# Closing products and norms by token, and a 31-tap convolution as dense products

## The chip, the cores and the metric

One NeuronCore of one Trainium2 chip. The metric is the device time of one execution in microseconds, median of three runs.

## The reference

512 tokens of 1024 channels, float32. Four blocks follow one another on one residual stream `x`; each adds two branches, `x = x + rms_norm(branch(rms_norm(x)))`. Blocks 1 and 2 have a mixer of three gated branches and a gated FFN with a 3-tap convolution (2 x 2816 hidden channels). Block 3 is a Conformer convolution module and an FFN, block 4 attention over dilated keys and an FFN. The parts that the change touches:

```python
def rms_norm(x, g):
    y = x * lax.rsqrt(jnp.mean(x * x, axis=-1, keepdims=True) + EPS)
    return y * g

def conformer_conv_module(h, w_in, b_in, dw, dw_b, ln_g, ln_b, w_out, b_out):
    u = h @ w_in + b_in
    u = u[..., :D_MODEL] * jax.nn.sigmoid(u[..., D_MODEL:])
    u = causal_dwconv(u, dw, dw_b)          # 31 taps, each channel by itself
    u = layer_norm(u, ln_g, ln_b)
    u = jax.nn.silu(u)
    return u @ w_out + b_out

x = x + rms_norm(y, post_gain)              # y: the closing product of a branch
h = rms_norm(x, pre_gain)                   # the next branch reads h
```

## The kernel before

**Layout.** Everything is held by feature: `x`, `y` and `h` are tiles of 128 features (partitions) x 8 feature tiles x 512 tokens. A product takes a 128 x 128 weight tile as stationary operand and streams the tokens. For accuracy weights and activations are split into a high and a low fp32r part, and `mm3` (line 318) makes each product of three matmuls: high x high, high x low, low x high. Attention, the convolution's taps, sums and transposes are plain fp32 matmuls.

**Weights** come in units of 8 tiles (128 x 1024, 512 KB) from one array in the order of a plan. `dma_to` (270) loads a unit on SP into one of three raw buffers, `split_to` (274) splits it, high on ACT (295) and low on DVE (296), into four rotating buffers or, where the plan says keep, into a second set of four. Units of two stages get the norm's gain multiplied in on GpSimd first (292).

**Order.** `spend` and `tick` keep a modelled clock: generators (lanes) for norms, softmaxes and taps are resumed when that clock passes the time that they asked for, so their instructions fall between the products. The framework below then orders each engine's instructions with the program's order as priority.

**Closing** (`closing`, 557). The last product of a branch (8 tiles of k, 8 tiles of output features) is done for tokens 0 to 255 and then for 256 to 511, 256 columns a matmul. Tiles 4 to 7 are kept for the second half, tiles 0 to 3 are loaded again. `close_tile` (519) evacuates each tile, ACT squares it, and GpSimd adds the squares up (381). In an FFN 14 of 22 k tiles were summed into `y` before, by `close_group` (497), 512 columns a matmul.

**Norms** (`norms`, 446). For each half: `rstd` (386) sums over features with 1-column matmuls (367), takes the reciprocal root in eleven small DVE instructions (`inv_sqrt`, 342, with the scaling at 393), and spreads it over the partitions with two PE transposes (358); `post_norm` (422) scales `y`, adds it to `x`, squares; a second `rstd`; `pre_norm` (403) scales `x` (413), ACT makes the high part (416), DVE and GpSimd the low part (418).

**Head** (`head`, 462). The first six output tiles of the next stage are done in halves too, so that half 0 can run while half 1 is normed: 288 matmuls of 256 columns.

**Convolution** (`conv_inputs`, 1156). For each of 16 half tiles the 31 taps are shared out by hand: ACT scales and GpSimd adds some (1201, 1202), PE does some as products with a diagonal matrix that ACT builds (1215, 1226), DVE does the rest (1245). `layer_norm` (1121) follows by half, with the same token sums.

## Time and profile before

| | us |
|---|---|
| median of 3 runs (3381.99 to 3386.56) | 3386.5 |
| the profiled execution's own time | 3382.53 |
| its span, first to last instruction | 3380.8 |
| PE busy (its matmuls) | 3249.0 |
| DVE, ACT, GpSimd busy | 1970.3, 1391.9, 725.0 |

The page gives one profiled execution. PE is TensorE's matmuls, PEld its weight loads, DVE VectorE, ACT ScalarE, POOL GpSimd, SP SyncE, which issues the loads. Matmuls overlap one another in the records, so a rate is read from a stretch and the number of matmuls in it, not from the duration of one; an fp32 matmul has two records, an fp32r matmul and a transpose one.

### The profile page before, as it was taken

Reading aid. Unit: us, or ns where it says so; the run is one execution under the profiler, and the core shown is the slowest. Engines: PE = TensorE matmul, PEld = TensorE weight load, DVE = VectorE, ACT = ScalarE, POOL = GpSimd, SP = SyncE. Lnnn points to the kernel's source line nnn. Section 1 sums busy time; section 2 is a strip of 40 time slices with the busy share of each in tenths; the row PEclk is TensorE's granted clock in tenths of the full one; section 3 lists DMA queues with packets and bytes.
Section 4 is the critical chain, followed back from the end, with each engine's and each line's share of the span. In section 5 each row is a group of like instructions: output and inputs, shape, how many; then the busy total and the mean of one; then the engine's idle time right before and its main releaser. Section 6 shows DMA issues by size and latency. Waiting matters only on the chain.

```text
span 3380.8 us, 45518 instructions
## 1 busy us (share of the span) xinstructions
PE 3249.0 (96%) x17626; PEld 2786.9 (82%) x17626; DVE 1970.3 (58%) x3697; ACT 1391.9 (41%) x2394; POOL 725.0 (21%) x753
## 2 busy tenths in 40 slices
PE   7999999999999999999998869999999999999998
PEld 7887888888988778988897668888888888898888
DVE  6655347455775443655567988455754454474555
ACT  4443244334454333444345655333433333353333
POOL 1122122000311212300024553000433333230001
PEclk9999999999999999999998979999999999999999
DMA  3111232222321223322231112232312222133222
GB/s 131 63 64 59 87 113 82 100 97 97 113 66 57 67 68 101 105 89 99 94 126 59 35 44 83 99 100 94 125 60 79 82 75 81 63 102 105 100 94 94
DMA packets 85848, 291.56 MB, mean 86 GB/s; under 512 B 9728, under 2 KB 16128, under 8 KB 85632
## 3 DMA queue, kind: packets, MB, share of 16 engines
q1 hardware_dynamic: 84480, 287.60, 25.6%
q8 instruction: 139, 2.28, 0.3%
q10 hardware_dynamic: 1152, 1.05, 0.1%
q14 instruction: 77, 0.63, 0.1%
HBM read 286.52 MB, written 2.10 MB: 85 GB/s over the span
## 4 chain that ended last, share of the span: by engine, by line
PE 81%; DVE 12%; POOL 2%; issue 2%; ACT 2%; DMA 1%; SPq 0%; POOLq 0%; DVEq 0%; ACTq 0%
PE mm L325 23%; PE mm L326 22%; PE mm L327 22%; DVE v L1245 4%; DVE w L296 2%; POOL acc L381 2%; PE z L326 1%; PE z L327 1%; PE z L325 1%; PE wpo L985 1%; PE ss L367 1%; DMA raw<-in_wall 1%; PE pt L862 1%; PE wsc L955 1%; PE dpo L1349 1%
## 5 line engine op out<-in xcount | busy, mean ns | idle before, releaser
L325 PE MATMUL mm<-hh,w 128*128 128x512 f32 (+1 forms) x2720 | 1058.5, 390 | 1.6 <-DVE cv L612 1.6
L326 PE MATMUL mm<-hl,w 128*128 128x512 f32 (+1 forms) x2720 | 1037.7, 382 | 0.0
L327 PE MATMUL mm<-hh,w 128*128 128x512 f32 (+1 forms) x2720 | 1037.4, 382 | 0.0
L296 DVE TENSOR_TENSOR w<-raw,w 128x1024 fp32r<-128x1024 f32 x468 | 605.1, 1293 | 439.7 <-ACT w L295 439.3
L295 ACT ACTIVATE w<-raw 128x1024 fp32r<-128x1024 f32 x468 | 492.5, 1053 | 274.1 <-PE mm L327 203.6
L325 PEld LDWEIGHTS mm<-hh,w 128*128 128x128 f32 x2720 | 513.1, 189 | 101.4 <-issue 12.9
L327 PEld LDWEIGHTS mm<-hh,w 128*128 128x128 f32 x2720 | 513.5, 189 | 98.7 <-issue 1.4
L326 PEld LDWEIGHTS mm<-hl,w 128*128 128x128 f32 x2720 | 514.5, 189 | 89.5 <-issue 2.4
L381 POOL TENSOR_TENSOR acc<-acc,sq 128x256 f32<-128x256 f32 x180 | 174.2, 974 | 1437.5 <-ACT sq L384 1412.2
L612 DVE SCALAR_TENSOR_TENSOR cg<-mm,vecs,cg 128x511 f32<-128x511 f32 (+1 forms) x176 | 131.9, 749 | 205.1 <-ACT cg L605 202.4
L325 PE MATMUL mm<-ah,w 128*128 128x512 f32 (+1 forms) x704 | 249.1, 357 | 1.1 <-ACT ah L632 0.9
L326 PE MATMUL mm<-al,w 128*128 128x512 f32 (+1 forms) x704 | 249.2, 354 | 0.0
L327 PE MATMUL mm<-ah,w 128*128 128x512 f32 (+1 forms) x704 | 248.7, 354 | 0.0
L612 DVE SCALAR_TENSOR_TENSOR cv<-mm,vecs,cv 128x511 f32<-128x511 f32 (+1 forms) x176 | 131.8, 749 | 100.3 <-ACT cv L605 97.8
L292 POOL TENSOR_TENSOR raw<-raw,vecs 128x1024 f32<-128x1024 f32 x72 | 146.1, 2030 | 199.5 <-DMA raw<-in_wall 193.9
L605 ACT ACTIVATE cg<-mm,vecs 128x512 f32<-128x512 f32 x88 | 68.4, 777 | 275.9 <-PE mm L327 275.9
L325 PEld LDWEIGHTS mm<-ah,w 128*128 128x128 f32 x704 | 135.0, 192 | 21.4 <-ACT ah L632 4.1
L326 PEld LDWEIGHTS mm<-al,w 128*128 128x128 f32 x704 | 135.4, 192 | 18.5 <-DVE al L633 1.6
L326 PE MATMUL mm<-hl,keep 128*128 128x256 f32 x512 | 146.9, 290 | 3.7 <-POOL hl L418 3.7
L327 PEld LDWEIGHTS mm<-ah,w 128*128 128x128 f32 x704 | 135.4, 192 | 17.2
L327 PE MATMUL mm<-hh,keep 128*128 128x256 f32 x512 | 146.6, 290 | 0.0
L325 PE MATMUL mm<-hh,keep 128*128 128x256 f32 x512 | 145.1, 294 | 1.5 <-ACT hh L416 1.5
(292 smaller groups left out, 5364.5 us busy)
## 6 DMA issues: line engine op xcount, KB each, us to landing
raw<-in_wall SPq DMA_DIRECT2D x532, 512.0 KB, 3.3
x<-in_x SPq DMA_DIRECT2D x4, 512.0 KB, 6.8
bt<-in_rpb SPq DMA_DIRECT2D x16, 128.0 KB, 2.0
out<-x SPq DMA_DIRECT2D x8, 128.0 KB, 1.8
out<-x ACTq DMA_DIRECT2D x8, 128.0 KB, 1.8
vecs<-in_vecs SPq DMA_DIRECT2D x1, 598.0 KB, 6.0
wpool<-in_w_pool SPq DMA_DIRECT2D x2, 256.0 KB, 2.7
cos<-in_cos SPq DMA_DIRECT2D x2, 256.0 KB, 2.9
```

The source lines that it names most:

```text
L292: nc.gpsimd.tensor_tensor(rows, rows, g[:, k0 : k0 + n, None].to_broadcast(list(rows.shape)), op=OP.mult)
L295: nc.scalar.activation(hi, raw, AF.Copy)
L296: nc.vector.tensor_tensor(lo, raw, hi.bitcast(F32), op=OP.subtract)
L325: nc.tensor.matmul(ps, wh, xh, start=first and i == 0, stop=False, **check)
L326: nc.tensor.matmul(ps, wh, xl, start=False, stop=False, **check)
L327: nc.tensor.matmul(ps, wl, xh, start=False, stop=stop, **check)
L367: self.nc.tensor.matmul(ps[:, i : i + 1], x[:, i * P : (i + 1) * P], self.ones, start=n == 0, stop=n == len(parts) - 1, skip_group_check=True,
L381: self.nc.gpsimd.tensor_tensor(parts[0], parts[0], sq, op=OP.add)
L605: nc.scalar.activation(o, ps, AF.Identity, scale=self.vec(taps + str(k0), f), bias=self.vec(cb, f))
L612: nc.vector.scalar_tensor_tensor(o[:, to], ps[:, of], self.vec(taps + str(k), f), o[:, to], op0=OP.mult, op1=OP.add,)
L862: nc.tensor.transpose(pt[:, k * P : (k + 1) * P], pm[:, k * P : (k + 1) * P], self.ident)
L1245: nc.vector.scalar_tensor_tensor(to, u, w, pss[n] if k == n_pool else to, op0=OP.mult, op1=OP.add)
```

## The change

Closing products have the token tile as stationary operand and stream 512 output columns, so `y` and `x` lie by token (128 tokens x 4 x 1024 features). All eight weight units of a closing stay for both halves. `x` is loaded and stored by token; the gains and one bias that act behind a closing product come as rows spread over the partitions by one load each (`row`). Norm sums are `accum_out` of ACT's squares, `x` gets its update in one DVE instruction a token tile, and the normed stream is transposed on PE into the layout of `h`. `head` takes its weight units one at a time and works tile by tile. The convolution is made of dense products: tokens are split in four residues by 4, a partition is a residue and one of 32 channels, and a 128 x 128 matrix that GpSimd builds from the taps and a 32 x 32 identity does four residues of one step; nine steps make the 31 taps. The input gets into that layout by 16 small copies a tile on SP's queue. Layer-norm sums come from `bn_stats` by token. `inv_sqrt`, `mm3`, `gemm`, `dma_to`, `split_to` and the FFN's own work are as before; SiLU and its split now follow a transpose back.

The diff, cut:

```diff
-BEGIN = 3
+CONV_M, CONV_PAD = 9, 8
+BEGIN = 4
+NORM_SUM, NORM_NEXT, NORM_TILE = (2.2, 3.6), 7.0, 1.1
...
     def closing(w, l, kt):
         _, last = out_groups(kt)
-        add(gemm_tiles(w, l, range(4), last))
-        add(gemm_tiles(w, l, range(4, 8), last), keep=True)
-        add(gemm_tiles(w, l, range(4), last))
+        for n, k in enumerate(last):
+            add(gemm_tiles(w, l, range(8), [k]), keep=n >= 4)
...
+    def rms(self, sums):
+        v = self.sm.tile([P, 2], F32, tag="var", name="var", bufs=2)
+        y = self.sm.tile([P, 2], F32, tag="rst", name="rst", bufs=4)
+        nc.vector.tensor_tensor(v, sums[:, :, 0], sums[:, :, 1], op=OP.add)
+        nc.vector.tensor_scalar(v, v, 1.0 / D, EPS, op0=OP.mult, op1=OP.add)
+        self.inv_sqrt(y, v)
+        return y
+
+    def square(self, x, total):
+        junk = self.sp.tile([P, S], F32, tag="junk", name="junk")
+        self.nc.scalar.activation(junk, x, AF.Square, accum_out=total)
+
+    def norms(self, h, banks, y, add, gain, bias, pre):
+        sums = self.sm.tile([P, 2, 2], F32, tag="sums", name="sums", bufs=4)
+        for i in range(2):
+            for n in range(2):
+                cols = slice(n * S, (n + 1) * S)
+                ps, to = banks[i][n], y[:, 2 * h + i, cols]
+                if add:
+                    nc.vector.tensor_tensor(to, to, ps, op=OP.add)
+                    self.square(to, sums[:, i, n : n + 1])
+                elif bias is not None:
+                    nc.vector.tensor_tensor(to, ps, bias[:, cols], op=OP.add)
+                    self.square(to, sums[:, i, n : n + 1])
+                else:
+                    self.square(ps, sums[:, i, n : n + 1])
+                    nc.vector.tensor_tensor(to, ps, gain[:, cols], op=OP.mult)
+                if add or bias is not None:
+                    nc.gpsimd.tensor_tensor(to, to, gain[:, cols], op=OP.mult)
+        rs = self.rms(sums)
+        for i in range(2):
+            t = 2 * h + i
+            for n in range(2) if pre is False else range(1):
+                cols = slice(n * S, (n + 1) * S) if pre is False else slice(0, D)
+                nc.vector.scalar_tensor_tensor(
+                    self.x[:, t, cols], y[:, t, cols], rs[:, i : i + 1], self.x[:, t, cols],
+                    op0=OP.mult, op1=OP.add,
+                )
...
+        yield from self.pre_norm(h, pre)
+
+    def pre_norm(self, h, gain, wait=(0.0, 0.0)):
+        sums = self.sm.tile([P, 2, 2], F32, tag="sums", name="sums", bufs=4)
+        for i in range(2):
+            for n in range(2):
+                cols = slice(n * S, (n + 1) * S)
+                self.square(self.x[:, 2 * h + i, cols], sums[:, i, n : n + 1])
+        rs = self.rms(sums)
+        xn = []
+        for i in range(2):
+            xn.append(self.sp.tile([P, D], F32, tag="xn", name="xn", bufs=2))
+            if i:
+                nc.vector.tensor_scalar(
+                    xn[i], self.x[:, 2 * h + i], rs[:, i : i + 1], None, op0=OP.mult
+                )
+            else:
+                nc.scalar.activation(xn[i], self.x[:, 2 * h + i], AF.Copy, scale=rs[:, i : i + 1])
+        yield NORM_SUM[h] + NORM_NEXT
+        for f in range(0, KD, 2):
+            pt = self.psum("b", "htp")
+            for j in range(2):
+                for i in range(2):
+                    nc.tensor.transpose(
+                        pt[:, (2 * j + i) * P : (2 * j + i + 1) * P],
+                        xn[i][:, (f + j) * P : (f + j + 1) * P], self.ident,
+                    )
...
+                for j in range(2):
+                    self.split_out(
+                        self.hh[:, f + j, at], self.hl[:, f + j, at], pt[:, j], self.vec(gain, f + j)
+                    )
+            self.ready[h] = f + 2
+            yield NORM_TILE
...
+    def mm3_rows(self, ps, x, w, first, last):
+        (xh, xl), (wh, wl) = x, w
+        nc.tensor.matmul(ps, xh, wh, start=first, stop=False)
+        nc.tensor.matmul(ps, xh, wl, start=False, stop=False)
+        nc.tensor.matmul(ps, xl, wh, start=False, stop=last)
...
+    def close_some(self, xs, units, banks, h, ks, which, first, last):
+        for k in ks:
+            rows = [half.rearrange("p n m -> p (n m)") for half in units[k]]
+            for i, n in which:
+                cols = slice((2 * h + i) * P, (2 * h + i + 1) * P)
+                self.mm3_rows(
+                    banks[i][n], (xs[k][0][:, cols], xs[k][1][:, cols]),
+                    [r[:, n * S : (n + 1) * S] for r in rows], k == first, k == last,
+                )
...
+            for k in range(done, KD):
+                units += self.take_units(gemm_tiles(w, l, range(8), [last[k]]))
...
+                self.close_some(xs, units, banks, 0, [k], every, 0, KD - 1)
+            self.spawn(self.norms(0, banks, y, add, gain, bias, pre))
+            banks = [[self.psum(tag, "mm") for tag in tags] for tags in (("a", "a"), ("a", "b"))]
+            order = (4, 5, 6, 7, 0, 1, 2, 3)
+            self.close_some(xs, units, banks, 1, order, every, 4, 3)
+            self.spawn(self.norms(1, banks, y, add, gain, bias, pre))
             if pre is not False:
                 self.head()
...
+        def matrices(j):
+            w = self.cf.tile([P, 4, CONV_M, 4, 32], F32, tag="cw", name="cw", bufs=2)
+            for i in range(4):
+                nc.gpsimd.tensor_tensor(
+                    w[:, i],
+                    taps[:, 4 * j + i, :, :, None].to_broadcast([P, CONV_M, 4, 32]),
+                    same[:, None, None, :].to_broadcast([P, CONV_M, 4, 32]),
+                    op=OP.mult,
+                )
...
+            up = cv.tile([P, 4, CONV_PAD + P], F32, tag="cup", name="cup", bufs=3)
+            nc.gpsimd.memset(up[:, :, :CONV_PAD], 0.0)
+            for i in range(4):
+                for q in range(4):
+                    nc.sync.dma_start(
+                        up[32 * q : 32 * q + 32, i, CONV_PAD:], u[32 * i : 32 * i + 32, q]
+                    )
...
+                for i in range(4):
+                    w = mats[j][:, i]
+                    for m in range(CONV_M):
+                        nc.tensor.matmul(
+                            ps[:, i * P : (i + 1) * P], w[:, m].rearrange("p a b -> p (a b)"),
+                            phased[j][:, i, CONV_PAD - m : CONV_PAD - m + P],
+                            start=m == 0, stop=m == CONV_M - 1, skip_group_check=True,
+                        )
...
+                if j + 2 < KD:
+                    matrices(j + 2)
+                vc = cv.tile([P, 4, P], F32, tag="vc", name="vc", bufs=2)
+                nc.vector.tensor_tensor(
+                    vc, ps.rearrange("p (i s) -> p i s", i=4),
+                    bias[:, 4 * j : 4 * j + 4, None].to_broadcast([P, 4, P]), op=OP.add,
+                )
...
+                for i in range(4):
+                    nc.tensor.transpose(pt[:, i * P : (i + 1) * P], vc[:, i], self.ident)
...
+                for q in range(4):
+                    nc.vector.bn_stats(stats[:, q, j], by[:, q])
```

## Rows read from the trace of the kernel before

**Rows 1.** The page's head, its part 1 (busy us, share of the span, instructions of each engine) and one line of its part 2 (the granted TensorE clock in 40 slices).

```profile
span 3380.8 us, 45518 instructions
...
PE 3249.0 (96%) x17626; PEld 2786.9 (82%) x17626; DVE 1970.3 (58%) x3697; ACT 1391.9 (41%) x2394; POOL 725.0 (21%) x753
...
PEclk9999999999999999999998979999999999999999
```

**Rows 2.** PE's waits over the whole execution: who waited for whom, us in total, times, longest.

```profile
PE bc L358 <- DVE rst L353: 29.3, 17, 10.2
PE taps L1226 <- DVE cu L1174: 24.3, 5, 10.4
PE ss L367 <- POOL acc L381: 16.3, 13, 4.1
PE mubc L358 <- DVE mu L1132: 13.8, 1, 13.8
```

**Rows 3.** Nine stretches (of the four plain closings with head the first, the second and the last): us from the span's start, length, then busy time (and instructions) of PE, PE's weight loads, DVE, ACT and GpSimd, granted clock, DMA share, GB/s.

```profile
0.00:61.00 61.00, 43.94 (x308) 43.00 (x309) 36.35 (x94) 24.43 (x46) 12.06 (x21) 0.92 0.46 155
470.00:564.00 94.00, 89.04 (x713) 88.12 (x712) 60.85 (x128) 45.71 (x89) 33.28 (x34) 0.96 0.30 97
848.40:942.10 93.70, 88.60 (x713) 87.55 (x712) 67.56 (x152) 42.49 (x80) 33.07 (x41) 0.96 0.33 108
1729.60:1823.70 94.10, 88.79 (x714) 87.62 (x713) 66.34 (x144) 42.16 (x78) 33.34 (x41) 0.96 0.30 100
1823.70:1998.20 174.50, 124.00 (x533) 102.96 (x531) 169.24 (x287) 114.38 (x280) 108.90 (x117) 0.86 0.10 34
1998.20:2102.10 103.90, 96.88 (x756) 94.41 (x757) 87.65 (x199) 53.41 (x109) 38.22 (x41) 0.95 0.27 87
2385.40:2487.70 102.30, 91.63 (x713) 90.24 (x712) 69.04 (x136) 38.59 (x72) 53.11 (x43) 0.93 0.30 96
2933.40:3036.80 103.40, 96.02 (x788) 94.34 (x787) 74.02 (x178) 51.73 (x110) 36.51 (x41) 0.98 0.26 88
3320.10:3380.80 60.70, 48.92 (x405) 48.14 (x403) 31.89 (x76) 16.22 (x27) 16.03 (x18) 0.92 0.29 92
```

**Rows 4.** PE alone in four stretches that hold one kind of matmul each: products of 512 columns, products of 256 columns, taps of the convolution in a long run, taps behind a wait. Columns as above, PE only.

```profile
2102.20:2145.40 43.20, 43.20 (x192) 1.00 0.31 100
860.70:873.60 12.90, 12.90 (x111) 1.00 0.50 168
1912.00:1956.70 44.70, 44.70 (x195) 0.94 0.06 17
1973.40:1981.60 8.20, 8.20 (x29) 0.68 0.00 1
```

**Rows 5.** Groups of instructions by line and shape, on ACT and then on DVE: count, busy us in all, mean ns of one, idle time before them.

```profile
L416 ACT ACTIVATE hh<-hf 128x256 fp32r<-128x256 f32 x128 | 51.3, 417 | 77.4 <-DVE hf L413 67.3 <-DVE hf L411 9.7
...
L829 ACT ACTIVATION_READ_ACCUMULATOR pm<-sc,smx,rq 128x1 f32 x64 | 12.5, 195 | 0.0
...
L726 ACT ACTIVATE rsq<-mm 128x512 f32<-128x512 f32 x10 | 5.9, 594 | 8.3 <-PE mm L327 8.2
...
L296 DVE TENSOR_TENSOR w<-raw,w 128x1024 fp32r<-128x1024 f32 x468 | 605.1, 1293 | 439.7 <-ACT w L295 439.3
...
L413 DVE SCALAR_TENSOR_TENSOR hf<-x,vecs,bc 128x256 f32<-128x256 f32 x112 | 49.3, 473 | 13.9 <-PE bc L358 13.8
...
L511 DVE TENSOR_TENSOR y<-y,mm 128x512 f32<-128x512 f32 x32 | 22.0, 686 | 38.1 <-PE mm L327 38.1
...
L1342 DVE COPY dps<-dpt 128x128 f32<-128x128 f32 x8 | 2.3, 292 | 15.4 <-PE dpt L1337 15.4
```

**Rows 6.** The same view for PE (taps of the convolution, token sums) and for PE's weight loads (one product of the attention over dilated keys).

```profile
L1226 PE MATMUL taps<-cu,cdiag 128*128 128x256 f32 x246 | 62.0, 415 | 24.3 <-DVE cu L1174 24.3
...
L367 PE MATMUL ss<-ones,acc 128*128 128x1 f32 x240 | 31.5, 250 | 18.6 <-POOL acc L381 16.3 <-ACT acc L384 2.3
...
L1349 PEld LDWEIGHTS dpo<-dps,dv 128*128 128x128 f32 x240 | 35.1, 191 | 3.4
```

**Rows 7.** PE alone in a stretch that holds nothing but fp32 products of 128 columns with weights of their own (two records each).

```profile
2939.40:2942.60 3.20, 3.20 (x31) 1.00 0.01 3
```

**Rows 8.** The tail in order of time: start us, us, engine, line. The last product, the first and last instruction of the last reciprocal root on DVE, the last update of x.

```profile
3367.25 0.28 PE L327 MATMUL mm<-ah,w 128*128 128x256 f32 x1
...
3369.37 0.16 DVE L393 TENSOR_SCALAR var<-ss 128x2 f32<-128x2 f32 x1 [1.37 <-PE ss L367]
...
3371.33 0.16 DVE L353 SCALAR_TENSOR_TENSOR rst<-nwa,rst 128x2 f32<-128x2 f32 x1
...
3377.39 0.72 POOL L437 TENSOR_TENSOR x<-x,y 128x256 f32<-128x256 f32 x1 [1.12 <-DVE y L433]
```

**Rows 9.** Two operations of GpSimd by source line: durations min/median/max in ns, first and last start.

```profile
L292 POOL TENSOR_TENSOR raw<-raw,vecs x72: 1891/1897/2987, 2404.5 to 2892.4; 128x1024 f32<-128x1024 f32 x72
...
L1033 POOL TENSOR_TENSOR macc<-macc,gate x32: 1280/1292/2177, 354.7 to 1353.7; 128x512 f32<-128x512 f32 x32
```

**Rows 10.** SP's queue at the start in order of time (start us, us that the issues took), and from the list of DMA issues the size and the median time to landing of the smallest regular load.

```profile
1.78 0.50 SPq L1483 DMA_DIRECT2D ident<-in_ident  x1
...
8.19 0.44 SPq L1494 DMA_DIRECT2D rot<-in_rot  x1
...
bt<-in_rpb SPq DMA_DIRECT2D x16, 128.0 KB, 2.0
```

More of the change, by code (lines that the diff above doesn't have):

```diff
@@ L422, in post_norm @@
-    def post_norm(self, h, y, gain, parts, last=False):
-        nc = self.nc
-        ys, xs = self.half(y, h), self.half(self.x, h)
-        bc = yield from self.rstd(parts)
-        squares = []
-        for f in range(KD):
-            if gain is None:
-                nc.vector.tensor_tensor(ys[:, f], ys[:, f], bc, op=OP.mult)
-            else:
-                nc.vector.scalar_tensor_tensor(
-                    ys[:, f], ys[:, f], self.vec(gain, f), bc, op0=OP.mult, op1=OP.mult
-                )
-            eng = nc.gpsimd if last and f % 3 == 1 else nc.vector
-            eng.tensor_tensor(xs[:, f], xs[:, f], ys[:, f], op=OP.add)
-            if last:
-                queue = nc.scalar if f % 2 else nc.sync
-                queue.dma_start(self.half(self.out, h)[:, f], xs[:, f])
-            else:
-                self.add_square(squares, f, xs[:, f])
-            yield POST_STEP
-        return squares
@@ L446, in norms, with row @@
-    def norms(self, h, y, post, pre, parts):
-        yield POST_WAIT[h]
-        squares = yield from self.post_norm(h, y, post, parts, pre is False)
-        if pre is not False:
-            yield PRE_WAIT[h]
-            yield from self.pre_norm(h, pre, squares)
+    def row(self, pool, name):
+        g = pool.tile([P, D], F32, tag=f"row{name}", name="row")
+        i = ROWS.index(name)
+        self.nc.sync.dma_start(g, self.t["rows"][i : i + 1].to_broadcast([P, D]))
+        return g
+    def rms(self, sums):
+        nc = self.nc
+        v = self.sm.tile([P, 2], F32, tag="var", name="var", bufs=2)
[4 more added lines that the diff above has]
+        return y
@@ L464, in head @@
         tiles = []
-        for _ in range(HEAD):
-            tiles += self.take(PLAN[self.n_unit][0])
-        pss = [self.psum("a" if i < 3 else "mm", "mm") for i in range(HEAD)]
+        pss = [self.psum("mm" if i < 3 else "a", "mm") for i in range(HEAD)]
         def some(h, which):
@@ L474, in some @@
                 for i in which:
-                    n = i * KD + k
-                    self.mm3(pss[i][:, cols], tiles[n : n + 1], hs[k : k + 1], k == 0, k == KD - 1)
-        pairs = [range(i, i + 2) for i in range(0, HEAD, 2)]
-        for which in pairs if start else [range(HEAD)]:
-            some(0, which)
-        for which in pairs:
-            some(1, which)
+                    if k == 0 and h == 0:
+                        tiles.append(self.take(PLAN[self.n_unit][0]))
+                    self.mm3(
+                        pss[i][:, cols], tiles[i][k : k + 1], hs[k : k + 1], k == 0, k == KD - 1
+                    )
+        step = 2 if start else 1
+        for h in range(2):
+            for i in range(0, HEAD, step):
+                some(h, range(i, i + step))
         self.headed = pss
@@ L560, in closing, with close_begin @@
+    def close_begin(self, w, l, xs):
+        banks = [[self.psum("mm", "mm"), self.psum("mm", "mm")], [self.psum("mm", "mm"), None]]
+        units = []
+        for k in range(BEGIN):
+            units += self.take_units(gemm_tiles(w, l, range(8), [k]))
+            self.close_some(xs, units, banks, 0, [k], [(0, 0), (0, 1), (1, 0)], 0, KD - 1)
+        return banks, units
+    def closing(self, w, l, xs, y, gain, pre, bias=None, ready=None, begun=None):
         groups, last = out_groups(len(xs))
-        begun = list(begun)
+        xs = [xs[k] for k in last]
+        add = bool(groups)
+        every = [(i, n) for i in range(2) for n in range(2)]
@@ L599, in ffn @@
         ):
-            y = fp.tile([P, KD, S], F32, tag="y", name="y")
+            y = fp.tile([P, 4, D], F32, tag="y", name="y")
+            gain = self.row(fp, post)
             def conv(ps, f, name):
@@ new lines, in conv @@
+            for q in range(4):
+                if q % 2:
+                    nc.scalar.activation(
+                        vt[:, q], vt[:, q], AF.Identity, scale=rs[:, q : q + 1], bias=sh[:, q : q + 1]
+                    )
+                else:
+                    nc.vector.tensor_scalar(
+                        vt[:, q], vt[:, q], mv[:, q, 0:1], rs[:, q : q + 1],
+                        op0=OP.subtract, op1=OP.mult,
+                    )
+        matrices(0)
+        matrices(1)
+        self.spawn(conv())
```

493 lines of the change are left out of this document (182 added, 311 removed).

## The prediction

> **What bounds the kernel now.** I read the page first, then who PE waits for, then a table of stretches, then single instructions. On the page [rows 1] the reader is to see that PE is busy 3249.0 of 3380.8 us at a granted clock near full: TensorE is the bound, and only two things can shorten the run: fewer PE slots, or fewer of the 131.8 us in which PE stands still. The waits [rows 2] say where it stands: for DVE's reciprocal roots (29.3 us) and GpSimd's sums of squares (16.3 us) in the norms that close a block, and in the convolution stage for DVE (24.3 and 13.8 us). The table of stretches [rows 3] then gives every place that the change touches: the start (0 to 61), seven stretches of closing product plus head (four plain ones of which the first, second and last take 94.0, 93.7 and 94.1 us, then 103.9, 102.3 and 103.4 us), the convolution's front (174.5 us, where PE is busy 124.0 and DVE 169.2, so DVE is the bound there) and the last closing with the tail (60.7 us). The ends are first instructions of a closing product and last ones of a head.
>
> The sum is made against the profiled execution: span 3380.8, time 3382.5 us. The median of the three runs is 3386.5, 4.0 more; I subtract the gain from the median. A measurement of this kernel can tell about 0.2% (7 us) from no change.
>
> **Closing products by token.** Before, a closing has 8 tiles x 8 k x 3 products x 2 halves = 384 of 256 columns; after, the token tile is stationary and 512 output columns stream: 2 halves x 8 k x 4 x 3 = 192. The pace comes from stretches that hold nothing else [rows 4]: 192 products of 512 in 43.2 us, 0.226 each, and 111 of 256 in 12.9 us, 0.118 each without those that overlap the edges. So 45.3 us become 43.4: -1.9 for each of 8 closings, -15. The same figure says that the two inner down-projections of an FFN, 168 products of 512 before and after, cost the same: 0. A sustained figure in the Trainium skill (TensorE: Matmul & The Clock Gate, Back-to-back issue gap), 131 ns for 512 columns in a stream of loads and products, would make a closing 25 us, as an estimate from that page, and this term -161 instead of -15; the trace differs, with 226 ns over 43 us, and the row stands.
>
> Four weight units less are fetched and split in each closing (they stay in their buffers for both halves). DVE's 1.29 us for each [rows 5] and ACT's share lie beside the half's 21.7 us of products; I count 0, and where that cover is thin now, their going is a gain.
>
> **Norms by token.** Removed from PE: with each of four root chains of a boundary 8 records of token sums and 2 broadcasts, 40 slots of about 0.11 us [rows 6, 7], 4.5 us. Added: 32 transposes of the normed stream at the pace of a 128-column product, 0.11 [rows 7], 3.5 us. Net -1.
>
> The larger part is the wait. PE work of a boundary before is 45.3 + 34.0 (the head: 288 products of 256) + 4.5 = 83.8 of 94, so 10 us are stalls and cold clock. After it is 43.4 + 34.0 + 3.5 = 80.9. The chain that must be hidden, from the end of a half's last bank: ACT squares of 512 from PSUM, 0.59 + 0.19 to read the sum [rows 5], the last at about 1.1; the root, measured as DVE instructions from 3369.37 to 3371.5 [rows 8] plus one add, 2.3; two x updates of 1024, at DVE's 1.29 for such a width [rows 5]; four squares of x (3.1, the first two beside the second update), the second root 2.3; the scaled copy 1.3; transposes 0.45; hh 0.42 and hl 0.47 per tile [rows 5]. That is 13.6 us to the first k and 17.4 to the eighth. In the FFNs GpSimd's gain product stands ahead of the x update: 1.29 for 128x512 [rows 9], four in a row, ending at 4.9, so about 1 us more. The cover: for half 0 the 21.7 us of half 1's products; for half 1 the head's half 0, 17.0, and 1.7 of transposes. Cover and chain are nearly equal, so the rest depends on what DVE and ACT do between: six head units are split in that time (7.7 us of DVE). I take 4 us of stalls for a boundary, between 0 (the chain always hidden) and 10 (as now). What is late next is hl on DVE. At an FFN's closing all four banks are wanted within 2 us where one half bank was wanted, so the last gate's evacuation delays it by about 1 us, in the 4.
>
> Boundary after: 80.9 + 4 = 85. Gains: four plain ones 9 each, 36; the one before the attention over dilated keys, whose head units GpSimd scales (1.89 each [rows 9]), 102.3 to 87, 15; the one with w_o 9; the convolution's own 103.9 to 91.5 (3.5 of transposes and 3 of cold clock more), 12. These hold the -15 and -7 above except the last closing's.
>
> Start: PE stands still for 17 of 61 us [rows 3]. x and the gains land as now; behind them stand 1.6 + 2.3 + 1.3 + 0.45 + 0.9 us (squares of one token tile, root, copy, transposes, hh and hl) to the first product, without sums over PE and without GpSimd's low parts. I take -6 (0 to -10). Tail: from the last product at 3367.5 to the end 13.3 us [rows 8]; after, 0.7 + 0.8 + 2.3 us to the root, four updates of 0.7 [rows 5], 2.7 from the last update to the end as now, and some 0.2 for GpSimd's last gain product: 9.5. That is -3.8, and with -1.9 of products about -5.5.
>
> The nine gain rows are one 512 KB load each on SP, which waits for the old stage's memory and stands ahead of weight loads. Three raw buffers ahead are 16 us of products. I count 0; if that cover is gone, it is at least the 2.0 us to landing of a small load [rows 10] at each stage's start, some 15 in all.
>
> **The convolution.** Removed: DVE's and GpSimd's taps, the diagonals, the token sums. Front after, on PE: ten projections (six are in the head) x 24 x 0.226 = 54.2; 8 x 4 x 9 = 288 fp32 products of 128 columns, two records each, 576 x 0.11 = 63.4 (31 such records in 3.2 us [rows 7]); 32 transposes 3.5. Against 246 records at 0.23, 56 us of taps now [rows 4, 6], PE gets more work, not less; the gain is the 50 us of idle [rows 3]. Three things can bring idle back.
> - GpSimd builds the matrices in 32 operations of 1152 elements, four for each tile. No such double broadcast is in the trace; the nearest, 1024 elements with one broadcast, takes 1.89 [rows 9], so 2.1 each. Bounds 1.5 and 8. The last group is due at about 116 us, from a start some 10 us before the head ends, so up to 3.9 each it costs nothing. Taken: 2.1, cost 0.
> - 16 small copies per tile on SP, at 0.43 to 0.5 us of queue each [rows 10], 7.2, and 2.0 to land, the time of the nearest small load [rows 10]. For the last tile: sigmoid and product 1.3 [rows 5], then 9.2, against 7.9 us of the convolution before it: 3 us of stall (0 to 8). Weight loads queue behind these copies on SP, which wait for DVE's u; three units of lead, 16 us, hide that.
> - The layer norm has no cover: bias add, transposes, copy, four bn_stats, four bn_aggr, root, two normalising passes of 1024, transposes, silu, split. With 0.29 us for 128 columns [rows 5] taken for a bn_stats, my sum is 14 us (bounds 9, if the passes and statistics take half, and 25, if they take twice as long and silu waits behind others).
> Front: 54.2 + 63.4 + 3.5 + 3 + 14 + 3 (cold) = 141: -33. The cold clock is shown by the taps behind the present 14 us wait: 1973.4 to 1981.6 ran at 0.68 of the clock [rows 4], some 2.5 us lost.
>
> **Sum:** 36 + 15 + 9 + 12 + 33 + 6 + 5.5 = 116.5. 3386.5 - 116.5 = 3270.
>
> **Rivals.**
> - *Stalls stay* (the norm chain is as late as now, 10 us a boundary): 6 less at each of 7, 42 less gain: 3312. For it: DVE carries root, updates, hl and splits in one queue, and roots are the largest wait now. Against: the chain loses the eight GpSimd sums and two trips through PE.
> - *The front gains nothing* (layer norm, copies or matrices keep it at 174): 3303.
> - *All hidden*, no stall at a boundary, layer norm 9: 4 x 7 + 5 + 6 more: 3231.
> - *Slower*: GpSimd's matrices become the bound. Front = 32 p - 10 (the early start) + 8 (the last convolution) + 14 = 32 p + 12; with the other gains of 83.5 the kernel is slower from p = 7.7 us, 6.7 ns per element where 1.85 is seen [rows 9]. At p = 9 it is 3428. For it: two zero strides and four dimensions are not in the trace.
> - *Weight loads show.* The 576 records each have their own weights, whose load takes 191 ns as a record [rows 6]. If a load could not run beside a product, 63.4 would be 576 x 0.30 = 172 us and the whole 3379. Such records at 0.11 [rows 7] speak against it. The Trainium skill (TensorE: Matmul & The Clock Gate, Part 3, under what overlaps) says that a load overlaps a product in flight only in another row group. By that rule this rival holds; the trace disagrees, with full-array products of changing weights at 0.11 us.
>
> **How the numbers follow.** Forecast 0.62 (3245 to 3300), stalls stay 0.16, front 0.08, all hidden 0.08, slower 0.05, loads 0.01. Range 3228 to 3322: it takes in the middle of every faster case and leaves out about 0.2 (the slower and loads cases, half of the best one, part of the stalls case). Faster by over 0.2%: 0.93; within: 0.02; slower: 0.05.
>
> **What would show it.** Right: closing plus head near 85 us in the table of stretches; no token sums or broadcasts on PE; the front near 141, with one PE gap of 10 to 18 us ahead of the closing; matrices at about 2.1 us; closing products at 0.226. Wrong: PE waiting for hl or the scaled copy by over 8 us a boundary (rival 1), for matrices or copies between convolutions (rivals 2 and 4), or 128-column records at 0.2 us and more (the last).

## The result

The median of the kernel after is 3289.2 us (3288.7 to 3289.7), of the kernel before 3385.9 us beside it: a ratio of 0.9717, 95% interval 0.9700 to 0.9734. I forecast 3270 with a range of 3228 to 3322: faster by 97 us where 116 were expected. Where the missing 20 us went is the subject of what follows.

### The profile page after: what moved, and what is told of

Same layout as the page of the kernel before. It is cut to its first block, busy times and chain, and to the rows that moved or that the text cites. A ratio compares the mean times of both kernels' runs of the same rounds, so it can differ in the third digit from the quotient of the medians.

```text
span 3287.3 us, 41615 instructions
## 1 busy us (share of the span) xinstructions
PE 3202.9 (97%) x16332; PEld 2683.4 (82%) x16332; DVE 1730.8 (53%) x3131; ACT 1271.3 (39%) x2056; POOL 489.9 (15%) x448
## 4 chain that ended last, share of the span: by engine, by line
PE 89%; DVE 6%; ACT 3%; issue 1%; DMA 0%; POOL 0%; SPq 0%; DVEq 0%; ACTq 0%; POOLq 0%
PE mm L325 19%; PE mm L327 19%; PE mm L326 18%; PE mm L511 6%; PE mm L512 6%; PE mm L513 6%; PE conv L1216 2%; ACT junk L382 2%; PE z L327 1%; PE z L325 1%; PE z L326 1%; PE wpo L998 1%; PE htp L444 1%; PE pt L875 1%; PE dpo L1350 1%
## 5 line engine op out<-in xcount | busy, mean ns | idle before, releaser
L296 DVE TENSOR_TENSOR w<-raw,w 128x1024 fp32r<-128x1024 f32 x436 | 569.4, 1306 | 467.0 <-ACT w L295 466.7
L295 ACT ACTIVATE w<-raw 128x1024 fp32r<-128x1024 f32 x436 | 459.1, 1053 | 285.9 <-PE mm L513 187.1
L403 POOL TENSOR_TENSOR y<-y,row 128x512 f32<-128x512 f32 x40 | 54.3, 1383 | 1310.5 <-ACT junk L382 1310.5
L625 DVE SCALAR_TENSOR_TENSOR cg<-mm,vecs,cg 128x511 f32<-128x511 f32 (+1 forms) x176 | 131.8, 749 | 212.9 <-ACT cg L618 209.9
L512 PE MATMUL mm<-w,ah 128*128 128x512 f32 x576 | 226.9, 394 | 0.0
L511 PE MATMUL mm<-w,ah 128*128 128x512 f32 x576 | 226.3, 393 | 0.0
L513 PE MATMUL mm<-w,al 128*128 128x512 f32 x576 | 225.9, 392 | 0.0
L327 PE MATMUL mm<-hh,keep 128*128 128x256 f32 x512 | 142.8, 281 | 0.1
L325 PE MATMUL mm<-hh,keep 128*128 128x256 f32 x512 | 142.0, 284 | 0.2 <-ACT hh L674 0.2
L511 PEld LDWEIGHTS mm<-w,ah 128*128 128x128 f32 x576 | 109.1, 189 | 23.7 <-issue 0.8
L513 PEld LDWEIGHTS mm<-w,al 128*128 128x128 f32 x576 | 109.4, 190 | 22.6
L512 PEld LDWEIGHTS mm<-w,ah 128*128 128x128 f32 x576 | 109.4, 190 | 22.5
```

What stands on the lines that cost most here:

```text
L295: nc.scalar.activation(hi, raw, AF.Copy)
L296: nc.vector.tensor_tensor(lo, raw, hi.bitcast(F32), op=OP.subtract)
L325: nc.tensor.matmul(ps, wh, xh, start=first and i == 0, stop=False, **check)
L327: nc.tensor.matmul(ps, wl, xh, start=False, stop=stop, **check)
L511: nc.tensor.matmul(ps, xh, wh, start=first, stop=False)
L512: nc.tensor.matmul(ps, xh, wl, start=False, stop=False)
```

## The profile after

The page's head, its part 1 and the granted clock, which answer to [rows 1]:

```profile
span 3287.3 us, 41615 instructions
...
PE 3202.9 (97%) x16332; PEld 2683.4 (82%) x16332; DVE 1730.8 (53%) x3131; ACT 1271.3 (39%) x2056; POOL 489.9 (15%) x448
...
PEclk9999999999999999999999989999899999999999
```

PE's idle time fell from 131.8 to 84.4 us, its busy time by 46. Who PE waits for (us in total, times, longest), against [rows 2]:

```profile
PE htp L444 <- ACT xn L437: 41.3, 14, 12.2
PE ltp L1137 <- DVE vt L1258: 9.1, 1, 9.1
PE mm L326 <- DVE hl L675: 6.9, 3, 2.4
...
PE mm L511 <- ACT keep L295: 2.5, 1, 2.5
```

The norms' token sums and broadcasts are gone. What is left is mostly one chain: the transposes (`htp`) wait for the scaled stream `xn`, which waits for DVE's two roots. The same nine stretches as in [rows 3], with the same columns:

```profile
0.00:53.30 53.30, 40.63 (x320) 38.90 (x321) 27.33 (x71) 29.35 (x55) 1.08 (x13) 1.00 0.51 175
462.50:547.70 85.20, 82.96 (x513) 73.67 (x512) 52.30 (x106) 41.65 (x75) 2.71 (x2) 1.00 0.27 89
830.60:921.00 90.40, 85.25 (x513) 75.41 (x512) 53.84 (x111) 41.63 (x80) 11.90 (x17) 0.96 0.27 89
1697.30:1787.30 90.00, 84.16 (x514) 74.02 (x513) 52.30 (x97) 39.99 (x72) 16.61 (x14) 0.98 0.32 102
1787.30:1928.20 140.90, 128.03 (x870) 116.22 (x869) 53.97 (x82) 33.24 (x41) 67.13 (x35) 0.95 0.24 74
1928.20:2019.50 91.30, 85.34 (x526) 75.12 (x526) 56.63 (x111) 43.92 (x77) 11.14 (x8) 0.98 0.16 53
2302.40:2404.80 102.40, 86.54 (x513) 76.59 (x512) 57.25 (x87) 36.24 (x63) 33.88 (x19) 0.90 0.25 81
2850.40:2947.60 97.20, 92.91 (x588) 81.99 (x587) 61.85 (x154) 46.69 (x94) 5.89 (x9) 0.98 0.23 77
3230.50:3287.30 56.80, 44.45 (x193) 35.71 (x191) 26.74 (x48) 11.63 (x23) 10.00 (x8) 0.93 0.18 63
```

| stretch | before | forecast | after | gain products and 11 scalings on DVE |
|---|---|---|---|---|
| start to the first head's end | 61.0 | 55 | 53.3 | 55.0 |
| first mixer: closing and head | 94.0 | 85 | 85.2 | 85.2 |
| first FFN | 93.7 | 85 | 90.4 | 84.1 |
| FFN ahead of the convolution | 94.1 | 85 | 90.0 | 84.2 |
| convolution's front | 174.5 | 141 | 140.9 | 140.8 |
| convolution's closing and head | 103.9 | 91.5 | 91.3 | 86.9 |
| FFN ahead of the dilated attention | 102.3 | 87 | 102.4 | 86.8 |
| dilated attention's | 103.4 | 94 | 97.2 | 97.1 |
| last closing and tail | 60.7 | 55.2 | 56.8 | 56.7 |

(The last column is an experiment, below.) Mixer, front and start met the forecast. The three FFN closings ahead of a head miss it by 5.4, 5.0 and 15.4 us: 26 together. They have in common what a mixer lacks: products of GpSimd during the norms. The latter FFN's second half, DVE and then GpSimd in order of time (start, us, engine, line; xN: N in a row):

```profile
2361.09 2.22 DVE L296 TENSOR_TENSOR w<-raw,w 128x1024 fp32r<-128x1024 f32 x1
2363.23 1.25 DVE L375 TENSOR_TENSOR var<-sums 128x2 f32<-128x2 f32 x1
2364.51 1.83 DVE L376 TENSOR_SCALAR var<-var 128x2 f32<-128x2 f32 x1
2366.38 1.22 DVE L347 TENSOR_SCALAR rst<-var 128x2 int32<-128x2 int32 x1
2367.63 1.21 DVE L351 TENSOR_TENSOR nwa<-rst 128x2 f32<-128x2 f32 x1
2368.87 1.82 DVE L352 SCALAR_TENSOR_TENSOR nwa<-nwa,var 128x2 f32<-128x2 f32 x1
2370.72 0.16 DVE L353 SCALAR_TENSOR_TENSOR rst<-nwa,rst 128x2 f32<-128x2 f32 x1
```

```profile
2360.93 3.53 POOL L403 TENSOR_TENSOR y<-y,row 128x512 f32<-128x512 f32 x2 [0.69 <-ACT junk L382]
2364.42 1.89 POOL L292 TENSOR_TENSOR raw<-raw,vecs 128x1024 f32<-128x1024 f32 x1
2366.28 2.54 POOL L403 TENSOR_TENSOR y<-y,row 128x512 f32<-128x512 f32 x2
2368.78 1.89 POOL L292 TENSOR_TENSOR raw<-raw,vecs 128x1024 f32<-128x1024 f32 x1
```

A root step on two numbers per partition takes 0.16 us while GpSimd is idle. Here five in turn take 1.21 to 1.83, and each ends within 0.1 us of the end of a GpSimd product (2364.5, 2366.3, 2367.6, 2368.8, 2370.7). The root takes 8.8 us instead of 2.3. The Trainium skill (SBUF — State Buffer, SBUF: two separate sides) gives a reason: DVE and GpSimd have one pair of ports in common, an exclusive lock for a whole instruction, for which a DVE instruction competes in a mode with two ports, or with two SBUF inputs while GpSimd reads SBUF. The lengths in these rows agree; the hold over twelve products in run 5, below, goes beyond it. My prediction did not weigh that page.

It is also told by the trace of before. Its chain of waits (start, us, what) has root steps of this kind in the same place:

```profile
2432.76 1.23 DVE rst L347
2434.01 1.82 DVE nwa L351
```

I had priced the root from the tail [rows 8], where nothing held it.

How late the chain may be is set by PE's order. In the first FFN the first transposes stand behind 154 closing products, that is behind 58 of half 1's 96. PE comes to them some 13 us after half 0's last product (which ends at 852.9) and waits there, although 38 products of half 1 are still to come:

```profile
869.22 0.98 PE L444 MATMUL htp<-ident,xn 128*128 128x128 f32 x4 [2.77 <-ACT xn L437]
```

The scaled stream is there 13.7 us after half 0's last product in the first mixer (PE waits 0.5 us), 16.3 in this FFN (2.8) and 21.3 in the FFN ahead of the dilated attention (7.8).

## The experiments

Theory H: GpSimd's products hold DVE's small instructions, the norm chain comes late, and PE's idle time is followed by a lower granted clock. Rival C: GpSimd's four products in a row are merely a longer chain. Stretches of every run are those of the table.

**1. Gain products on DVE.**

```diff
-                    nc.gpsimd.tensor_tensor(to, to, gain[:, cols], op=OP.mult)
+                    nc.vector.tensor_tensor(to, to, gain[:, cols], op=OP.mult)
```

> The kernel after, with the gain products of the closings that accumulate or add a bias on DVE instead of GpSimd (four FFNs and the conformer). Theory H (a small DVE instruction that starts while GpSimd runs a product is held until that product ends: root steps of 1.2 us where 0.16 is normal, and the idle of PE behind it is followed by a cold clock): root steps at 0.16 to 0.17 us everywhere but in ffn2; ffn0 90.4 and ffn1 90.0 become 85 to 86.5; the conformer's closing and head 91.3 becomes 89; ffn2 102.4 becomes 97; the tail loses 2 us; in all about -18, 3271 us (3266 to 3276). Rival C (the FFNs lose only because four GpSimd products in a row end 0.75 us after the sums that the root waits for): at most 1 us for each half, ffn0 and ffn1 88.5, in all -6 to -9, 3281 us. Rival N (DVE is short of time in these boundaries, so that four products of 0.7 more for each half on it cost as much as they give): 3287 to 3295.

Measured: 3262.9 us (3262.8 to 3263.1), 26 less. Four stretches: the two FFNs, the convolution's closing, the FFN ahead of the dilated attention.

```profile
831.40:915.50 84.10, 83.36 (x513) 73.66 (x512) 53.59 (x119) 41.88 (x80) 0.87 (x9) 1.00 0.29 96
1691.90:1776.10 84.20, 83.47 (x514) 73.72 (x512) 52.14 (x105) 40.30 (x72) 5.66 (x6) 1.00 0.33 107
1916.80:2003.90 87.10, 86.37 (x527) 76.19 (x526) 56.39 (x119) 44.28 (x77) 0.00 (x0) 0.98 0.16 55
2286.80:2377.90 91.10, 83.84 (x513) 74.19 (x512) 56.25 (x95) 35.92 (x63) 22.95 (x11) 0.98 0.28 91
```

Each goes below H's number, the last by 11.3 where 5 were expected, and the whole lies below H's range. PE's busy time falls too (85.25 to 83.36 in the first): the same products at a granted clock of 1.00 instead of 0.96. The root's first step (L347) takes at most 0.17 us anywhere in this run. But this run does not give the price of the hold, for PE's order changed with it: in the first FFN the first transposes now stand behind 178 closing products instead of 154. The chain has become longer (four adds and four products queue on DVE ahead of the root), and the scaled stream is there 18.9 us after half 0's last product (end 853.7) instead of 16.3; yet PE does not wait for it:

```profile
872.58 0.66 PE L444 MATMUL htp<-ident,xn 128*128 128x128 f32 x4
```

The other FFN and the convolution's closing have the same order and the same times. So 16 of these 26 us, those of the first three stretches, come with a chain that is better covered and not shorter, and neither H's sum nor C's describes the run. Why the order came out otherwise stays open, and the kernel after with its transposes later and GpSimd as it is was not tried.

**2. The same time on GpSimd, with one input.**

```diff
-                    nc.gpsimd.tensor_tensor(to, to, gain[:, cols], op=OP.mult)
+                    for _ in range(2):
+                        nc.gpsimd.tensor_scalar(to, to, self.ones[:, 0:1], 1.0, op0=OP.mult, op1=OP.mult)
```

> The kernel after, with each GpSimd gain product of 1.26 us (two inputs from SBUF) replaced by two GpSimd products with a column of ones (one input, 0.69 us each as such a form shows elsewhere in the trace); the gain is left out. GpSimd is as long on the chain as before. Theory H as it stands (any product of GpSimd holds DVE until it ends): a root step is held for up to 0.7 us instead of 1.25, ffn0 and ffn1 within 1 us of 90, in all 3285 to 3290. Variant H2 (only a GpSimd product with two inputs from SBUF holds DVE): root steps at 0.16, ffn0 and ffn1 at 88, in all 3278 to 3282. Rival C (chain length alone): ffn0 and ffn1 at 90 to 91, 3289 to 3292, whatever the root steps do.

This kernel leaves the gain out. Measured: 3287.0 us (3284.9 to 3292.9), as the kernel after; the two FFNs 90.7 and 89.2. PE's order is that of the kernel after. The first FFN's root in this run:

```profile
856.27 0.64 DVE L347 TENSOR_SCALAR rst<-var 128x2 int32<-128x2 int32 x1
856.94 0.62 DVE L351 TENSOR_TENSOR nwa<-rst 128x2 f32<-128x2 f32 x1
857.60 0.63 DVE L352 SCALAR_TENSOR_TENSOR nwa<-nwa,var 128x2 f32<-128x2 f32 x1
858.26 0.16 DVE L353 SCALAR_TENSOR_TENSOR rst<-nwa,rst 128x2 f32<-128x2 f32 x1
```

A product of about half the length (0.70 us) holds a step half as long, and five steps are held where three were. Two inputs on GpSimd's side are not needed (H2 falls). The time fits C as well, which says nothing of the steps.

**3. Products that nobody waits for, in the closings that had none.**

```diff
                     nc.vector.tensor_tensor(to, ps, gain[:, cols], op=OP.mult)
+                    junk = self.sp.tile([P, S], F32, tag="gjunk", name="gjunk")
+                    nc.gpsimd.tensor_tensor(junk, to, gain[:, cols], op=OP.mult)
```

> The kernel after, with four GpSimd products of 128x512 with two inputs for each half added to the closings that have none (two mixers and the dilated attention's); each reads the finished tile and writes a tile that nobody reads, so that nothing on the chain waits for them. Theory H: root steps of 1.2 us appear in these three boundaries, mixer0 and mixer1 85.2 become 87.5 to 90, the dilated one 97.2 becomes 100; in all +7 to +14, 3296 to 3303. Rival C (only work that the chain waits for counts): 85.2 and 97.2 unchanged within 0.7, 3288 to 3290.

Measured: 3304.5 us (3303.6 to 3307.4), 15.3 more. The two mixers and the dilated attention's closing:

```profile
462.70:553.80 91.10, 84.73 (x513) 74.97 (x512) 56.77 (x106) 41.57 (x75) 13.90 (x10) 0.98 0.26 83
1335.60:1425.00 89.40, 82.92 (x514) 73.69 (x513) 56.61 (x106) 41.69 (x75) 14.09 (x10) 1.00 0.25 85
2859.30:2962.40 103.10, 94.77 (x588) 83.22 (x587) 66.19 (x154) 46.58 (x94) 17.08 (x17) 0.97 0.22 72
```

They are +5.9, +4.2 and +5.9 us, by work that no instruction reads, and the whole lies just above H's range. PE's order in the three is that of the kernel after, and ACT's squares take 0.60 us in both. Two held steps of the first mixer's first root, and the products over them:

```profile
488.44 1.15 DVE L347 TENSOR_SCALAR rst<-var 128x2 int32<-128x2 int32 x1
489.82 1.14 DVE L352 SCALAR_TENSOR_TENSOR nwa<-nwa,var 128x2 f32<-128x2 f32 x1
```

```profile
485.51 5.43 POOL L403 TENSOR_TENSOR gjunk<-y,row 128x512 f32<-128x512 f32 x4 [18.01 <-PE mm L515]
```

That root takes 4.9 us instead of 2.3, and PE's first wait for the scaled stream is 3.1 us instead of 0.5. This parts the theories: the hold is shown, and is somewhat dearer than I expected. C falls as the whole cause.

**4. The 11 scalings of weight units on DVE as well.**

```diff
-                nc.gpsimd.tensor_tensor(
+                eng = nc.vector if self.n_kv < 11 else nc.gpsimd
+                self.n_kv += 1
+                eng.tensor_tensor(
                     rows, rows, g[:, k0 : k0 + n, None].to_broadcast(list(rows.shape)), op=OP.mult
```

> As the gain products on DVE, and also the 11 scalings of raw weight units that fall into ffn2's closing and head on DVE instead of GpSimd (128x1024, 1.89 us each on GpSimd). Theory H: without a GpSimd product in that stretch its root steps are at 0.16 us and ffn2's stretch goes from 102.4 to 86 to 88; in all about -32, 3257 us (3253 to 3262). Rival C: ffn2's stretch is long because 11 x 1.89 us of GpSimd's scaling delays the weight units, and DVE's 1.2 us for each delays them as much: 97 to 100, 3268 to 3273.

Measured: 3258.8 us (3258.0 to 3260.3). The FFN ahead of the dilated attention took 91.1 in run 1 and takes 86.8 now, the number that H gave and not C's. But again the chain is not shorter: the scaled stream is there 22.5 us after half 0's last product, where the kernel after had 21.3, because splits and scalings on DVE stand between the root's steps. PE has all 192 closing products ahead of its first transposes here, and waits 0.4 us instead of 7.8. The steps themselves are no longer held. Group rows of DVE's start of the root (count, busy us, mean ns), first after, then this run:

```profile
L347 DVE TENSOR_SCALAR rst<-var 128x2 int32<-128x2 int32 x32 | 15.7, 492 | 1.1
```

```profile
L350 DVE TENSOR_SCALAR rst<-var 128x2 int32<-128x2 int32 x32 | 5.4, 170 | 1.0
```

**5. The matrices of the convolution built twice.** `for _ in range(2):` ahead of the product that builds `w[:, i]`.

> The kernel after, with each of the 32 GpSimd operations that build the convolution's matrices issued twice, so that a matrix group costs 4.57 us instead of 2.29. By the formula of the prediction's slower rival (front = 32 p + 12) the front goes from 141 to 158: 3306 us. Theory B (buffers set the pace: the four operations of a tile have the 19.4 us of a tile's projections and convolution, so they are free up to 4.85 each): the front stays at 140 to 143, 3288 to 3293. Theory H adds that GpSimd's longer work holds DVE's weight splits and products of the front, which does not show as long as PE has its units in time.

Measured: 3325.1 us (3324.7 to 3330.3), front 176.6. All three numbers miss. PE's waits in the front, then the instruction behind the first of them on DVE:

```profile
PE ctp L1234 <- DVE vc L1227: 19.2, 3, 17.6
PE conv L1217 <- POOL cw L1177: 11.2, 5, 4.7
```

```profile
1830.30 25.64 DVE L296 TENSOR_TENSOR w<-raw,w 128x1024 fp32r<-128x1024 f32 x1 [0.85 <-ACT w L295]
```

A weight split of 1.2 us took 25.64, through twelve GpSimd products in a row, and the bias add behind it made PE wait 17.6 us. It ended 1.15 us after GpSimd had come to a memset, about its own length:

```profile
1784.72 70.14 POOL L1177 TENSOR_TENSOR cw<-taps,same 128x1152 f32<-128x1152 f32 x32
1854.79 0.18 POOL L1199 MEMSET cup<- 128x32 f32 x2
```

**6. Closing products in halves of 256 columns**, on run 4's kernel:

```diff
-        nc.tensor.matmul(ps, xh, wh, start=first, stop=False)
...
+        for c in (slice(0, HS), slice(HS, S)) if halves else (slice(0, S),):
+            nc.tensor.matmul(ps[:, c], xh, wh[:, c], start=first, stop=False, **check)
```

(the other two matmuls are cut in the same way; the closings' sums differ from those of run 4, and the run is read for its time.)

> The kernel with gain products and unit scalings on DVE (3258.8 us), with the closing products of all 8 closings in 256 columns again, 384 instead of 192 each; everything else by token as before. By the prediction's term (0.118 against 0.226 us): each closing alone 43.3 becomes 45.3, the whole +15 us, 3274 (3271 to 3277). Rival P (a 256-column product with the new operand order or with the same operand twice in turn runs at exactly half the 512-column pace, 0.113): 0 to +3, 3259 to 3262. Where part of the closing's time covers stalls behind it, the whole is up to 3 less than either.

Measured: 3273.0 us (3271.4 to 3274.5), +14.2: the term of 15 has the right size, and P falls. PE alone in the kept units' part, 99 products of 512 in the kernel after and 193 of 256 here:

```profile
474.80:496.90 22.10, 22.10 (x99) 1.00 0.17 54
```

```profile
474.90:497.80 22.90, 22.90 (x193) 1.00 0.15 45
```

That is 0.223 and 0.119 us each (those that overlap the edges counted), at the same clock; by their starts they are 0.227 and 0.120 us apart. At that pace halves cost 2.5 us a closing. The mixers show it (2.5 and 2.9 us), the FFNs 1.1 to 1.4, since part of it covers waits there.

**7 and 8. The last 48 products of half 1 bank after bank**, on the kernel after, and on run 4's:

```diff
-            self.close_some(xs, units, banks, 1, order, every, 4, 3)
+            self.close_some(xs, units, banks, 1, order[:4], every, 4, 3)
+            for bank in every:
+                self.close_some(xs, units, banks, 1, order[4:], [bank], 4, 3)
```

> The kernel after, GpSimd as it is, with only the order of the last 48 products of half 1 in each closing changed: bank after bank instead of k after k, so that the four banks end 2.7 us apart and not within 2 us. Theory H: GpSimd's products of the first three banks are done before the root, which is then held by one product at most: 1 to 2.5 us less in the four FFNs and the conformer, 1 to 2 less in the tail; 3289 becomes 3277 to 3284. Rival Q (what is late is DVE's and ACT's own queue, four adds and four squares behind the last product): the mixers gain as well, 1 us or more each, where they have stalls: 3270 to 3277. Rival R (the weight buffers come free later and the head waits for them): 3289 or more.

> The same order of the last 48 products, on the kernel with gain products and unit scalings on DVE (3258.8 us, where no root is held). The tail: 12.4 us from the last product to the end becomes 10 (one add, one square and one gain product ahead of the root instead of a queue of four). A boundary has less than 1 us of waiting left for half 1 and gains 0 to 1. In all -3 to -8, 3254 us. Rival R (the head waits for weight buffers): 3259 or more, with the tail still 2 shorter.

Measured on the kernel after: 3285.5 us (3280.6 to 3288.4), just above H's range, with runs that spread over 8 us. In its profile the FFN stretches get shorter by 3.4, 1.4 and 0.6 us and the convolution's by 2.0, the mixers get longer by 0.4: as H has it, not Q, but small where unit scalings remain. On run 4's: 3256.8 us (3255.4 to 3259.3), 2.0 less, short of the 3 to 8 expected; the two kernels' runs overlap. The last closing and tail take 54.9 instead of 56.7.

**9 and 11. Pauses for GpSimd in run 5's kernel.** First a memset of a tile of its own behind each matrix operation, then one into the operation's own tile ahead of it:

```diff
                 for _ in range(2):
+                    nc.gpsimd.memset(w[:, i, 0, 0, :], 0.0)
                     nc.gpsimd.tensor_tensor(
```

> The kernel with every matrix operation issued twice (3325.1 us, front 176.6, of which 17.6 us is PE behind one DVE weight split that took 25.6 us and ended when GpSimd came to a memset), with a memset of 128x32 behind each of the 64 operations. Theory S (a held DVE instruction gets in only when GpSimd pauses or runs something that reads nothing from SBUF; in an unbroken run of products it can stay held): no split is longer than 5 us, the 17.6 us wait of PE goes, and the front is 159 to 163 although GpSimd has about 8 us more to do: 3306 to 3313. Rival G (the front is late because GpSimd has 146 us of matrices to build, and the split's time only shows it): 177 to 185, 3325 to 3335.

> As the kernel with every matrix operation issued twice, with a memset of 128x32 ahead of each of the 64 operations that writes into the same tile, so that it can't be moved out of the run of products (in the run before, 31 of the memsets came together behind the products, 18 products stayed unbroken, and the split took 25.64 us again). Theory S (a held DVE instruction gets in at a pause of GpSimd): no DVE split over 5 us, PE's wait of 14 to 18 us for the bias add gone, front 159 to 166, 3306 to 3313. Rival G (the amount of GpSimd's work is what is late): front 176 to 185, 3325 to 3335.

The first (3326.9 us, 3325.5 to 3330.3) did not do what it was to: 31 of the memsets came together ahead of 32 unbroken products and 31 more behind them, and a split took 25.64 again. (The expectation of the second counts 18 of these 32, those behind 1818 us.) It says nothing against S. In the second at most three products follow one another: 3317.8 us (3316.7 to 3320.0), front 167.8. No split takes over 3.10 us, and PE's waits are other ones:

```profile
PE conv L1218 <- POOL cw L1177: 10.4, 6, 3.1
...
PE conv L1218 <- POOL cw L1178: 2.8, 3, 1.1
...
PE ctp L1235 <- DVE vc L1228: 1.6, 2, 0.8
```

The wait of 17.6 us has gone, which is S. The time lies between S and G: the amount of work (146.3 us of GpSimd) takes part of it back, with 13.2 us of waits for matrices and a granted clock of 0.89 in the front instead of 0.95. That it was the memsets, and not the shorter rows of products, is not shown.

**10. All 72 unit scalings on DVE**, on run 8's kernel.

> The kernel with banks in turn, gain products and 11 unit scalings on DVE (3256.8 us), with the other 61 scalings of raw weight units, which fall where PE is 99% busy, on DVE too: 61 products of 1.89 us on GpSimd, which hold DVE's instructions of that stage, become 61 of about 1.2 on DVE. Theory H with cover (a hold costs only where nothing covers the chain): within 3 us of 3256.8 either way. Rival (holds cost everywhere): -10 or more.

Measured: 3253.6 us (3252.4 to 3254.9), 3.2 less, just outside the 3 us that H with cover allowed and far from -10. It is the fastest of all: 0.9616 of before (0.9602 to 0.9630).

## Why the prediction was right and where it failed

- **Closing products, right.** 0.226 us was forecast, 0.227 is seen from start to start, and run 6 gives 14.2 us for undoing the term of 15. The sustained figure of the Trainium skill (TensorE: Matmul & The Clock Gate, Back-to-back issue gap) named in the prediction, 131 ns, does not show here either.
- **Four microseconds of stalls, right where GpSimd is idle.** The mixers took 85.2 for 85 (80.9 of work and 4.3 of stalls, of which the record shows 2.2 as idle time of PE), and the FFNs 84.1 and 84.2 in run 1, with GpSimd out of the chain and PE's order changed. The chain behind it was only nearly right: its terms as named add up to 14.0 us with the four squares one after another, or 12.7 with two beside the second update, where I wrote 13.6; in the first mixer the first `hl` ends 15.3 us after half 0's last product.
- **The failed step** is the FFNs' chain and its cover: "GpSimd's gain product stands ahead of the x update ... so about 1 us more", with "102.3 to 87" as the same mistake at its largest, and "for half 0 the 21.7 us of half 1's products". I added GpSimd's time to the chain and kept the root at 2.3 us beside it; the first root of an FFN's half takes 4.6 to 5.1 there, and two roots ahead of the dilated attention 8.4 and 8.8. And half 0's cover is not 21.7 us but some 13, the 58 products that PE has ahead of the transposes. Run 3, with PE's order as it was, gives 4.2 to 5.9 us a boundary for the hold, in place of the 1; the two plain FFNs missed by 5.4 and 5.0. The FFN ahead of the dilated attention missed by 15.4, and PE's two waits there are 7.8 and 8.1 us; how they divide between hold and order is open. What runs 1 and 4 gave back (6.3, 5.8, 4.2 and 15.6 us) is both together. A part is the clock behind the stall: in the first FFN PE stood nearly still for 3.3 us, and over the next 22 instructions the granted clock was 0.70:

```profile
866.00:869.30 3.30, 0.53 (x3) 1.00 0.63 236
869.30:875.00 5.70, 5.70 (x22) 0.70 0.40 125
```

- **The convolution's closing, right by luck.** 91.5 forecast, 91.3 measured, but 87.1 in run 1: the 3.5 and 3 us that I added for transposes and clock look about 4 too many, and PE's waits of 2.8, 2.3 and 0.8 us for the normed stream, 0.7 of which are left in run 1, filled them.
- **The front, right in the sum (141), by errors that cancel.** Products came as worked out: the 72 records of a tile start within 7.92 us. Of the 20 us beside the 121 of work, the layer norm's waits are about 11 (9.1 and 2.2; I said 14), the copies' stall is 0 (I said 3), and PE's busy time is 7 above the sum, at a clock of 0.95 (I said 3). Matrices took 2.29 us each on average, 2.13 in the median (I said 2.1), and cost PE nothing.
- **The slower rival's formula, 32 p + 12, wrong;** the limit of 3.9 us for free matrices was not tried. At p = 4.57 the formula gives 158, the chip 176.6, or 167.8 with pauses. GpSimd's load costs more than its own lateness. The rival was rightly unlikely, but its point of decision, 7.7 us, was probably set too high.
- **Start** -7.7 for -6, but it takes 52.9 to 55.8 us in the profiles of the other runs, which don't change it. **Tail** -3.9 for -5.5: its root took 4.5 us under GpSimd (3276.75 to 3281.25) instead of 2.3. With the gain products on DVE the tail is no shorter (56.7): its root is back at 2.3 us, but starts 3.9 us after the last product instead of 1.8, behind four adds and four products; bank after bank gives 1.8.
- **The dilated attention's closing** is 3 to 4 us over the forecast in every kernel that adds nothing to it, 2.5 of it PE's wait for ACT's split of the kept units; why that comes late was not tried.
- **The rivals.** "Stalls stay" came half true, in the FFNs alone and by another mechanism. "Weight loads show" fell: 72 records with weights of their own start 0.112 us apart.
- **Sum.** The three FFN stretches are 25.8 us short of the forecast, the dilated attention's 3.2, the tail 1.6. The start (1.7), the stretches between (4.5) and rounding in the table (1.4) give 7.6 back: 23.0, which is 116.5 less the 93.5 of the two spans. With GpSimd out of the way, and PE's transposes later, the same change gives 3258.8, 11 below the forecast.

## What to carry to other kernels

Before work is placed on GpSimd, look at what DVE does in the same microseconds: each step of a chain of tiny DVE instructions that falls under a GpSimd instruction can be held to its end, however small the step is. Whoever waits for the chain pays it; where other work covers the chain, a hold costs little (run 10). The cover is the work that stands ahead of the waiting instruction in its engine's order, not all the work that depends on nothing: read from the trace where the waiting instruction stands, and look again after every edit, for an edit on another engine can move it (run 1). Price a chain from a place with the same neighbours, not from the quietest one in the trace. A row whose mean is several times what the same step takes elsewhere (492 against 170 ns here) is the sign.

## What the hardware showed unexpectedly

- A held DVE instruction can stay held for more than GpSimd's current instruction: 25.64 us through twelve products in a row (runs 5 and 9), up to a memset both times; with memsets of 0.12 us in between no split took over 3.10 us (run 11). Earlier in the same rows of products, and in rows of eight, DVE got in between two of them; what decides that is open.
- One-input GpSimd products hold DVE as two-input ones do: steps of 0.62 to 0.64 us under products of 0.70 (run 2). DVE's TENSOR_SCALAR with one tensor input is held as well (1.22 us).
